# A two-layer decoder trunk with mixture of experts: the convolution's columns requested first, routing and gathering without the norm's scale and shift

## The chip, the cores and the metric

The kernel runs on one core of a Trainium2 chip. Its engines work side by side, each through its own instructions in order: TensorE (PE in the profile, its weight loads PEld), VectorE (DVE), ScalarE (ACT), GpSimd (POOL) and SyncE (SP), which here only issues transfers. ScalarE and GpSimd issue a few transfers too, in line with their other work. The metric is the device time of one execution in microseconds (us), as the median of several runs.

## What is computed

Two layers over 256 tokens of width 1024, all in float32. Layer 0 mixes tokens with a gated causal convolution of 31 taps, layer 1 with causal attention of 12 heads; in both, 4 more heads attend to 256 memory tokens. After each mixer stand an output projection, a residual with a norm, a mixture of 32 experts of which each token uses two, and a second residual with a norm.

```python
y = jnp.dot(jnp.concatenate([y_mix, y_mem], axis=-1), w_o[i])
x = layer_norm(DEEPNORM_ALPHA * x + y, ln1_g[i], ln1_b[i])
f = hierarchical_moe(x, w_rg[i], b_rg[i], w_re[i], b_re[i], w_gate[i], w_up[i], w_down[i])
x = layer_norm(DEEPNORM_ALPHA * x + f, ln2_g[i], ln2_b[i])
```

`layer_norm` is `(x - mean) * rsqrt(var + eps) * g + b`. The router takes the best of 4 groups and then the best two of its 8 experts; a token's output is the weighted sum of `silu(x @ w_gate) * (x @ w_up) @ w_down` over its two experts. Every expert has 6 MB of weights (three matrices of 2 MB), and all 32 are read in each layer: 403 of the 443 MB that the program reads.

## The kernel before

**Buffers and the order of loads.** Weights and large intermediate tiles share one pool, `big`, of 22 buffers of 128 x 2048 floats (1 MB each). `want` puts a load on a list, and `pump` hands the loads out in the order of that list, on SyncE's queue, as soon as the count of free buffers lets it; `act` takes a buffer for an intermediate tile and `free` gives it back; `done` gives back a weight tile. A buffer is given again as soon as it is free, in no fixed rotation. The list is: six tiles of convolution weights, the memory tokens, key and value weights, the four tiles of `w_o`, the gains and shifts of the first norm (`gb`, 1 MB: the 8 KB row repeated on 128 partitions), then the experts in the order of `_plan`, six tiles each (gate, up, down, two halves). Layer 1's list follows in the same manner. Eight semaphores are given in turn to all transfers that SyncE and ScalarE issue; a transfer that is given one in use waits at its issue until the earlier transfer on it has landed, and with it waits everything behind it on its engine.

**Static and dynamic experts.** Four experts (`s` in `_plan`) are fixed, so their 24 tiles can be loaded before the routing is known. The other 28 are taken in order of their token counts: their loads wait for the gate `("moe", l)`, opened when the router's result `eid` stands. `_plan` has twelve units, 0 to 11, each with one, two or four experts on 128 slots: two units with two static experts, then units of four, one, two, four, one, two, four, two, four and four experts.

**The start.** `raw` (the transposed x) comes in two halves. `parted` (L389) splits it into a rounded part, cast on ScalarE, and a remainder, subtracted on VectorE. `conv_layer` then takes its tile `cv_`, requests the per-channel columns (taps, bias, norm) into it on ScalarE's queue (L552), and begins to split the convolution's weights with `Feed` (L344 cast, L345 remainder) for the projection matmuls (L405). The gated product h goes to HBM and comes back in shifted copies `hs` (L597, L617, on GpSimd's queue); 28 of the 31 taps then run on TensorE (L626), three on VectorE (L607, L610). The token rows `xs` for the residual are loaded after the router's weights (L685, on SyncE) and multiplied into the accumulator by `residual` (L499 through L496).

**Norm and routing.** `moe` (L1043) takes the norm's statistics of token tile 0 (`norm_stats`), applies the norm with gains and shifts on VectorE (`norm_apply`, L519 and L520), then does the statistics of tile 1. `turn_tokens` transposes a tile for the router, `route` multiplies it by the router's weights (L1084) and adds a bias row (L1086), `choose` finds group and experts on VectorE (L1091 to L1106). Token tile 1 is already routed from rows without gains and shifts: its weights are `rwg`, the router's weights times the gains (GpSimd, L1049), and its bias row has the shifts' product added (L1135, L1144). GpSimd multiplies and adds gains and shifts to its two halves meanwhile (L1140, L1141). Then `Gather` multiplies the rows by one-hot matrices (L929) for the first unit; its result is copied from PSUM in two halves (L940). Later units do the same with `gather` (L950, copies at L952 through `evac`, which alternates ScalarE and VectorE).

**The experts.** For each expert, `gate` and `up` (L974), `turn` (L1004) and `down` (L1026); the next unit's gather stands between `up` and the previous expert's `down`. `scatter` adds a unit's result to the accumulator, and at the end of units 5, 6, 8 and 10 (`REST`) `residual` adds alpha times the normalised rows. After unit 11 comes the second norm.

## Time and profile before

| | |
|---|---|
| median of 3 runs | 1175.22 us (1174.49 to 1183.54) |
| the profiled execution | 1182.57 us, of it 1180.9 us span |
| mean granted TensorE clock | 0.947 |
| TensorE busy | 1028.2 us (87%), weight loads 722.3 us (61%) |
| VectorE, ScalarE, GpSimd busy | 366.4, 210.5, 60.6 us |
| moved by transfers | 447.16 MB, 379 GB/s over the span |

The span runs from the first to the last instruction. A row of a timeline gives start, duration, engine, line and operation with the tiles it writes and reads, merged where equal instructions follow each other; in brackets stands how long the engine was idle before it and what ended that. SPq and ACTq are transfer issues. A busy TensorE is not one at its peak, since matmuls are pipelined. PEclk is the share of the full clock that was granted: 1.00 is 2.4 GHz, 0.50 is 1.2 GHz.

### The profile page before, as it was taken

Reading aid. Unit: us, or ns where it says so; the run is one execution under the profiler, and the core shown is the slowest. Engines: PE = TensorE matmul, PEld = TensorE weight load, DVE = VectorE, ACT = ScalarE, POOL = GpSimd, SP = SyncE. Lnnn points to the kernel's source line nnn. Section 1 sums busy time; section 2 is a strip of 40 time slices with the busy share of each in tenths; the row PEclk is TensorE's granted clock in tenths of the full one; section 3 lists DMA queues with packets and bytes.
Section 4 is the critical chain, followed back from the end, with each engine's and each line's share of the span. In section 5 each row is a group of like instructions: output and inputs, shape, how many; then the busy total and the mean of one; then the engine's idle time right before and its main releaser. Section 6 shows DMA issues by size and latency. Waiting matters only on the chain. (4 is left out here: it accounts for less than half of the span.)

```text
span 1180.9 us, 26574 instructions
## 1 busy us (share of the span) xinstructions
PE 1028.2 (87%) x11292; PEld 722.3 (61%) x11292; DVE 366.4 (31%) x936; ACT 210.5 (18%) x456; POOL 60.6 (5%) x152
## 2 busy tenths in 40 slices
PE   1998999999889998866589998999997999996775
PEld 1986766665565575544469986666545656654542
DVE  3576832221121121111065765222211211221103
ACT  2314411111010010001044532011010111110000
POOL 1440200000000000000020002000000000000001
PEclk9999989999999999889899997999998999997777
DMA  9686969999999999999997386999999999999994
GB/s 381 235 282 265 347 251 419 424 424 426 425 424 425 427 424 425 426 426 425 425 427 271 108 293 252 384 425 424 426 427 422 425 427 425 424 426 425 426 425 177
DMA packets 63656, 447.16 MB, mean 379 GB/s; under 512 B 7656, under 2 KB 8040, under 8 KB 10280
## 3 DMA queue, kind: packets, MB, share of 16 engines
q1 hardware_dynamic: 61640, 439.73, 90.2%
q0 software_dynamic: 1600, 4.90, 1.5%
q8 instruction: 92, 1.51, 0.5%
q10 hardware_dynamic: 288, 0.73, 0.2%
q14 instruction: 36, 0.29, 0.1%
HBM read 442.87 MB, written 2.46 MB: 377 GB/s over the span
## 5 line engine op out<-in xcount | busy, mean ns | idle before, releaser
L974 PE MATMUL pb<-w,xg 128*32 128x128 f32 (+2 forms) x6528 | 400.1, 323 | 87.3 <-DMA w<-in_w_gate_dram 51.0
L974 PEld LDWEIGHTS pb<-w,xg 128*32 128x32 f32 (+2 forms) x6528 | 276.6, 123 | 208.9 <-issue 82.8
L1026 PE MATMUL pb<-w,hT 128*32 128x256 f32 (+1 forms) x1600 | 157.5, 432 | 7.8 <-DMA w<-in_w_down_dram 3.1
L1026 PEld LDWEIGHTS pb<-w,hT 128*32 128x32 f32 (+1 forms) x1600 | 74.5, 116 | 62.9 <-issue 36.5
L1031 ACT COPY o<-pb 32x256 f32<-32x256 f32 (+2 forms) x104 | 43.2, 416 | 367.1 <-DVE o L1031 232.5
L405 PE MATMUL pb<-xT,hl 128*128 128x256 f32 x672 | 86.0, 290 | 25.8 <-ACT hl L344 25.6
L1031 DVE COPY o<-pb 32x256 f32<-32x256 f32 (+2 forms) x104 | 49.8, 478 | 177.6 <-PE pb L1026 157.7
L998 DVE TENSOR_TENSOR h<-pb,h 128x128 f32<-128x128 f32 (+2 forms) x64 | 22.9, 358 | 253.8 <-PE pb L974 246.8
L405 PEld LDWEIGHTS pb<-xT,hl 128*128 128x128 f32 x672 | 84.0, 198 | 27.3 <-ACT hl L344 25.6
L496 PE MATMUL pa<-o,pt 128*128 128x512 f32 x192 | 92.7, 628 | 3.5 <-DVE o L1031 2.0
L950 PEld LDWEIGHTS pb<-oh,xn 128*128 128x128 f32 x704 | 80.6, 192 | 7.4 <-issue 7.4
L950 PE MATMUL pb<-oh,xn 128*128 128x128 f32 x704 | 84.0, 278 | 0.0
L345 DVE TENSOR_TENSOR hl<-w,hl 128x1024 fp32r<-128x1024 f32 x53 | 63.1, 1221 | 36.0 <-ACT hl L344 33.1
L496 PEld LDWEIGHTS pa<-o,pt 128*128 128x128 f32 x192 | 37.7, 207 | 44.5 <-issue 32.4
L344 ACT CAST hl<-w 128x1024 fp32r<-128x1024 f32 x54 | 54.7, 1053 | 33.3 <-DMA w<-in_memT_dram 19.3
L992 ACT ACTIVATE h<-pb 128x128 f32<-128x128 f32 (+2 forms) x64 | 21.2, 331 | 195.9 <-PE pb L974 195.0
L128 POOL TENSOR_SCALAR lmv<-lmv 128x1 f32<-128x1 f32 x8 | 1.7, 216 | 1027.7 <-DVE lmv L506 1026.0
L496 PE MATMUL pa<-hl,y 128*128 128x512 f32 x192 | 46.0, 395 | 0.0
L125 DVE COPY hT<-pb 128x128 f32<-128x128 f32 (+2 forms) x32 | 11.4, 358 | 105.1 <-PE pb L1004 81.2
L123 ACT COPY xg<-pb 128x512 f32<-128x512 f32 x22 | 12.9, 586 | 160.4 <-PE pb L950 160.4
L496 PEld LDWEIGHTS pa<-hl,y 128*128 128x128 f32 x192 | 35.5, 188 | 8.0 <-issue 0.5
L1238 DVE TENSOR_SCALAR ow<-iota,sm,sw 128x128 f32<-128x128 f32 x96 | 26.8, 343 | 19.2 <-PEq L1395 13.3
(229 smaller groups left out, 705.9 us busy)
## 6 DMA issues: line engine op xcount, KB each, us to landing
w<-in_w_gate_dram SPq DMA_DIRECT2D x128, 1024.0 KB, 19.5
w<-in_w_up_dram SPq DMA_DIRECT2D x128, 1024.0 KB, 19.5
w<-in_w_down_dram SPq DMA_DIRECT2D x128, 1024.0 KB, 19.5
w<-in_moba_w_in_dram SPq DMA_DIRECT2D x10, 1024.0 KB, 18.4
w<-in_w_o_dram SPq DMA_DIRECT2D x8, 1024.0 KB, 19.8
w<-in_conv_w_in_dram SPq DMA_DIRECT2D x7, 1024.0 KB, 15.4
w<-in_gains_dram SPq DMA_DIRECT2D x4, 1024.0 KB, 12.4
hs<-hd POOLq DMA_DIRECT2D x24, 142.0 KB, 3.2
```

The source lines that it names most:

```text
L123: nc.scalar.copy(o, i)
L344: nc.scalar.copy(hi, src)
L345: eng.tensor_sub(lo, src, hi.bitcast(F32))
L405: nc.tensor.matmul(o, lhsT=lhs(a, j), rhs=rhs(b, j), start=k == 0, stop=k == 3 * n - 1)
L496: nc.tensor.matmul(self.at[t][half], lhsT=lhsT, rhs=rhs, start=start, stop=stop)
L950: nc.tensor.matmul(p_[:, j - jj], lhsT=now(t, j), rhs=oh[t], start=t == 0, stop=t == NT - 1)
L974: nc.tensor.matmul(o_[b * n:(b + 1) * n, :], lhsT=self.xs[:, j, :], rhs=wj[:, pairs(b) if fw == P else slice(b * fw, (b + 1) * fw)], start ...
L992: nc.scalar.activation(self.h[:, :fw], g_, AF.Silu)
L998: nc.vector.tensor_mul(self.h[:, :fw], u_, self.h[:, :fw])
L1026: nc.tensor.matmul(ds[0][b * n:(b + 1) * n, :dw], lhsT=chunk(c), rhs=wd(c, b * dw, (b + 1) * dw), start=c == 0, stop=c == 3)
L1031: (nc.scalar.copy if 2 * b >= m else nc.vector.tensor_copy)(o[lo:lo + n, b * D // m:(b + 1) * D // m], ds[b] if nb == 1 else ds[0][b * n:( ...
L1238: nc.vector.tensor_scalar(o_[:, t], iota, sm[:, i:i + 1], sw[:, 4 + i:5 + i], op0=OP.is_equal, op1=OP.mult)
```

## The change

Five edits stand in it.

1. The tile `cv_` is taken, and the convolution's columns requested on ScalarE's queue, right after the two loads of `raw`.
2. The token rows `xs` are requested after the second `taps`, ahead of the last convolution block.
3. Both token tiles are normalised without gains and shifts (`plain`: half 0 on VectorE, half 1 on ScalarE). `rwg` is made in `router_load`; both tiles are routed with it and with the corrected bias row, whose product stands ahead of the first routing product. GpSimd's four operations on tile 1 are gone.
4. Gains and shifts are applied to the gathered, transposed copies, where they are one value per partition: `lift` reads PSUM in eight pieces of 128 x 128, four on ScalarE and four on VectorE, for each gather.
5. `gb` of the first norm is requested ahead of unit 7's experts. After unit 7 GpSimd makes `x1`, the rows with gains and shifts, in a buffer of its own (eight operations on 128 x 512), and `residual` reads it after units 8, 9, 9 and 10.

```diff
-REST = (5, 6, 8, 10)
+LIFT = 7
+REST = (8, 9, 9, 10)
...
     def want_moe(l):
-        for experts in plan:
+        for g, experts in enumerate(plan):
+            if g == LIFT:
+                want(("gb", l, 1), load_gb(2 * l))
...
+    cv_ = act("cv")
+    ncol = MC * (CW + 5), MC * 32
+    nc.scalar.dma_start(cv_[:, MC * S:MC * S + sum(ncol)], conv_cols)
     for b in range(3):
         for i in range(2):
             want(("cv", b, i), load(conv_w_in, 2 * b + i))
...
-    want(("gb", 0, 1), load_gb(0))
     want_moe(0)
...
-        rws.append((rw, rws_[:, 1], gbc))
+        rwg = rws_[:, 1]
+        nc.gpsimd.tensor_mul(rwg, rw, gbc[:, :J, None].to_broadcast([P, J, NL]))
+        rws.append((rw, rwg, gbc))
...
-        cv_ = act("cv")
...
-        nc.scalar.dma_start(cols, conv_cols)
...
         taps(1)
+        for t in range(NT):
+            for half in range(2):
+                nc.sync.dma_start(xn[t][half], xs[t, half])
         glu(2)
...
         router_load(0)
-        for t in range(NT):
-            for half in range(2):
-                nc.sync.dma_start(xn[t][half], xs[t, half])
         feed.ahead(2)
...
+    def lift(xg, p_, gbc, half):
...
+        for i in range(4):
+            j = 4 * half + i
+            g, b = gbc[:, j:j + 1], gbc[:, J + j:J + j + 1]
+            if half:
+                nc.vector.tensor_scalar(xg[:, j], p_[:, i], g, b, op0=OP.mult, op1=OP.add)
+            else:
+                nc.scalar.activation(xg[:, j], p_[:, i], AF.Identity, bias=b, scale=g)
...
-            evac(xg[:, jj:jj + 4], p_)
+            lift(xg, p_, gbc, jj // 4)
...
+        def plain(t):
...
+            nc.vector.tensor_scalar(xn[t][0], acc.at[t][0], mv[:, 0:1], mv[:, 2:3], op0=OP.subtract, op1=OP.mult)
+            nc.vector.scalar_tensor_tensor(mv[:, 3:4], mv[:, 0:1], -1.0, mv[:, 2:3], op0=OP.mult, op1=OP.mult)
+            nc.scalar.activation(xn[t][1], acc.at[t][1], AF.Identity, bias=mv[:, 3:4], scale=mv[:, 2:3])
...
-        gb = held(("gb", l, 1))
-        norm_apply(acc, 0, mv0, gb)
-        mv1 = norm_stats(acc, 1)
+        plain(0)
+        mv = norm_stats(acc, 1)
...
-        for half, eng in ((0, nc.gpsimd), (1, nc.gpsimd)):
-            o = xn[1][half]
-            g, b = gain(gb, half)
-            eng.tensor_mul(o, o, g)
-            eng.tensor_add(o, o, b)
-        done(("gb", l, 1))
...
+            if g == LIFT and end:
+                x1 = act("x1").rearrange("p (k d) -> p k d", k=4)
+                gb = held(("gb", l, 1))
+                for k in range(4):
+                    g_, b_ = gain(gb, k % 2)
+                    nc.gpsimd.tensor_mul(x1[:, k], xn[k // 2][k % 2], g_)
+                    nc.gpsimd.tensor_add(x1[:, k], x1[:, k], b_)
+                done(("gb", l, 1))
+            for k in range(4):
+                if g == REST[k] and end:
+                    residual(acc, k // 2, k % 2, x1[:, k])
```

ScalarE's first instructions before; `raw` is x, `hl` the split weights, and the brackets name the semaphores that a row waits for (DMAHW0 to DMAHW7 are the eight of the transfers):

```order
L394 ACT_TABLE_LOAD
L394 CAST xT<-raw 128x1024 [waits DMAHW0_49]
L552 DMA cv<-in_conv_cols_dram 128x408 [waits DMAHW0_49]
L344 CAST hl<-w 128x1024 [waits DMAHW2_49]
L344 CAST hl<-w 128x1024
L344 CAST hl<-w 128x1024 [waits DMAHW3_49]
```

and after, where the request waits for nothing and stands ahead of the casts:

```order
L254 DMA cv<-in_conv_cols_dram 128x408
L400 ACT_TABLE_LOAD
L400 CAST xT<-raw 128x1024 [waits DMAHW0_49]
L350 CAST hl<-w 128x1024 [waits DMAHW3_49]
L350 CAST hl<-w 128x1024
L350 CAST hl<-w 128x1024 [waits DMAHW4_49]
```

The request has moved from behind the wait for a transfer's semaphore to the head of the queue.

SyncE's queue from the four loads of `w_o` on, before; `xn` are the token rows, the rows of `gains` the 1 MB of the first norm:

```order
L183 DMA w<-in_w_o_dram 128x2048 x4
L189 DMA w<-in_gains_dram 128x2048
L213 DMA w<-in_w_gate_dram 128x2048 x2
L213 DMA w<-in_w_up_dram 128x2048 x2
L213 DMA w<-in_w_down_dram 128x2048 x2
L213 DMA w<-in_w_gate_dram 128x2048 x2
L327 DMA rbias<-in_b_rg_dram 1x4
L328 DMA rbias<-in_b_re_dram 1x32
L329 DMA rw<-in_w_r_dram 128x320
L331 DMA gbc<-in_gain_cols_dram 128x16
L685 DMA xn_72<-in_xs_dram 128x512
```

and after:

```order
L184 DMA w<-in_w_o_dram 128x2048 x4
L646 DMA xn_72<-in_xs_dram 128x512
L646 DMA xn_73<-in_xs_dram 128x512
L646 DMA xn_74<-in_xs_dram 128x512
L646 DMA xn_75<-in_xs_dram 128x512
L214 DMA w<-in_w_gate_dram 128x2048 x2
L214 DMA w<-in_w_up_dram 128x2048 x2
L214 DMA w<-in_w_down_dram 128x2048 x2
L214 DMA w<-in_w_gate_dram 128x2048 x2
L214 DMA w<-in_w_up_dram 128x2048
```

The token rows now stand right behind `w_o`, and the load of the gains has left this place.

VectorE from the statistics of token tile 0 (`lst`) to the first choice (`gm`, `gi`), before:

```order
L505 BN_STATS lst<-pa 128x6 x2
L506 BN_AGGR lmv<-lst 128x2
L519 SCALAR_TENSOR_TENSOR xn_72<-pa,lmv,w 128x512
L520 SCALAR_TENSOR_TENSOR xn_72<-xn_72,lmv,w 128x512
L519 SCALAR_TENSOR_TENSOR xn_73<-pa,lmv,w 128x512
L520 SCALAR_TENSOR_TENSOR xn_73<-xn_73,lmv,w 128x512
L505 BN_STATS lst<-pa 128x6 x2
L506 BN_AGGR lmv<-lst 128x2
L1128 SCALAR_TENSOR_TENSOR lmv<-lmv 128x1
L1130 TENSOR_SCALAR xn_74<-pa,lmv 128x512
L1077 COPY x1T<-pb 128x512
L1091 MAX gm<-lg 128x8
```

and after:

```order
L511 BN_STATS lst<-pa 128x6 x2
L512 BN_AGGR lmv<-lst 128x2
L1065 TENSOR_SCALAR xn_72<-pa,lmv 128x512
L1066 SCALAR_TENSOR_TENSOR lmv<-lmv 128x1
L511 BN_STATS lst<-pa 128x6 x2
L512 BN_AGGR lmv<-lst 128x2
L1065 TENSOR_SCALAR xn_74<-pa,lmv 128x512
L1066 SCALAR_TENSOR_TENSOR lmv<-lmv 128x1
L1151 TENSOR_TENSOR rows<-rbias,pb 1x40
L1096 COPY x1T<-pb 128x512
L1110 MAX gm<-lg 128x8
```

Four operations on tile 0 have become one with a small one behind it, and the bias row (`rows`) now stands ahead of the first choice.

## Rows read from the trace of the kernel before

**Rows 1.** The page, part 2: GB/s moved in 40 equal slices of the span.

```profile
GB/s 381 235 282 265 347 251 419 424 424 426 425 424 425 427 424 425 426 426 425 425 427 271 108 293 252 384 425 424 426 427 422 425 427 425 424 426 425 426 425 177
```

**Rows 2.** The chain that ended last: start us, us, what.

```profile
1143.53 19.41 DMA w<-in_w_down_dram
```

**Rows 3.** Timeline: start us, us, engine, line, what. The queue's release in layer 0.

```profile
160.00 3.02 SPq L213 DMA_DIRECT2D w<-in_w_down_dram  x2
```

**Rows 4.** Timeline of the start, with [idle before <-releaser].

```profile
9.40 0.33 SPq L183 DMA_DIRECT2D w<-in_conv_w_in_dram  x1
24.09 0.38 ACTq L552 DMA_DIRECT2D cv<-in_conv_cols_dram  x1
24.50 5.78 ACT L344 CAST hl<-w 128x1024 fp32r<-128x1024 f32 x6 [19.27 <-DMA w<-in_memT_dram]
25.60 31.77 PE L405 MATMUL pb<-xT,hl 128*128 128x256 f32 x240 [25.60 <-ACT hl L344]
```

**Rows 5.** Waits of the DMA queue's own engine, 0 to 30 us: us, times, longest.

```profile
SPq L183 <- DMA w<-in_conv_w_in_dram: 13.6, 6, 3.0
```

**Rows 6.** DMA issues: engine, count, KB each, median us to landing.

```profile
hs<-hd POOLq DMA_DIRECT2D x24, 142.0 KB, 3.2
cv<-in_conv_cols_dram ACTq DMA_DIRECT2D x1, 204.0 KB, 7.0
rw<-in_w_r_dram SPq DMA_DIRECT2D x2, 160.0 KB, 12.6
```

**Rows 7.** Timeline of the convolution: first shifted copies, first tap matmuls.

```profile
44.72 4.49 POOL L617 DMA_DIRECT2D hs<-hd  x8 [1.57 <-ACT hl L344]
57.30 3.01 PE L626 MATMUL pb<-hs,wdg 128*32 128x256 f32 x52
```

**Rows 8.** Timeline of layer 0's residual matmuls.

```profile
99.82 5.40 PE L496 MATMUL pa<-xn,alpha 128*128 128x512 f32 x8 [3.25 <-DMA xn<-in_xs_dram]
```

**Rows 9.** Timeline of layer 1's residual matmuls.

```profile
693.67 2.84 PE L496 MATMUL pa<-xn,alpha 128*128 128x512 f32 x6
```

**Rows 10.** Timeline of layer 0's routing, both token tiles.

```profile
142.91 0.74 PE L1135 MATMUL pb<-rw,gbc 128*1 128x40 f32 x16
144.16 1.10 DVE L1096 TENSOR_TENSOR pen<-iota,gi 128x4 f32<-128x4 f32 x1
145.19 1.26 POOL L1140 TENSOR_TENSOR xn<-xn,w 128x512 f32<-128x512 f32 x1
145.29 1.21 DVE L1098 SCALAR_TENSOR_TENSOR me<-pen,lg 128x32 f32<-128x32 f32 x1
147.06 0.81 DVE L1104 TENSOR_TENSOR m<-iota,ei 128x64 f32<-128x64 f32 x1
148.16 0.21 PE L1083 MATMUL pb<-msum,upper_b 128*128 128x32 bf16 x1 [3.06 <-DVE msum L1106]
149.76 3.78 PE L929 MATMUL pb<-oh,xn 128*128 128x128 f32 x16
150.57 0.16 DVE L1096 TENSOR_TENSOR pen<-iota,gi 128x4 f32<-128x4 f32 x1
150.77 0.19 DVE L1098 SCALAR_TENSOR_TENSOR me<-pen,lg 128x32 f32<-128x32 f32 x1
151.52 0.23 DVE L1104 TENSOR_TENSOR m<-iota,ei 128x64 f32<-128x64 f32 x1
```

**Rows 11.** The page, part 5: groups, busy us, mean ns of one.

```profile
L992 ACT ACTIVATE h<-pb 128x128 f32<-128x128 f32 (+2 forms) x64 | 21.2, 331 | 195.9 <-PE pb L974 195.0
L1238 DVE TENSOR_SCALAR ow<-iota,sm,sw 128x128 f32<-128x128 f32 x96 | 26.8, 343 | 19.2 <-PEq L1395 13.3
```

**Rows 12.** Waits of the DMA queue's own engine, 330 to 460 us.

```profile
SPq L213 <- PE pb L974: 1.2, 4, 0.4
```

**Rows 13.** Stretches: us, busy by engine, granted clock (PEclk), DMA share, GB/s.

```profile
150.00:152.00 2.00, 2.00 (x10) 2.00 (x11) 1.67 (x11) 0.45 (x3) 0.00 (x0) 0.50 0.93 348
714.00:716.00 2.00, 1.57 (x8) 1.53 (x8) 0.28 (x1) 0.94 (x3) 0.44 (x1) 0.62 1.02 430
```

More of the change, by code (lines that the diff above doesn't have):

```diff
@@ L496, in add, with residual @@
             nc.tensor.matmul(self.at[t][half], lhsT=lhsT, rhs=rhs, start=start, stop=stop)
-    def residual(acc, t, half):
-        acc.add(t, half, alpha, xn[t][half])
+    def residual(acc, t, half, x=None):
+        acc.add(t, half, alpha, xn[t][half] if x is None else x)
     def norm_stats(acc, t):
@@ L544, in conv_layer @@
         free()
-        cv_ = act("cv")
         cv = cv_[:, :MC * S].rearrange("p (c s) -> p c s", c=MC)
-        npc, nwr = MC * (CW + 5), MC * 32
-        cols = cv_[:, MC * S:MC * S + npc + nwr]
-        pct = cols[:, :npc].rearrange("p (c k) -> p c k", c=MC)
-        wrc = cols[:, npc:].rearrange("p (c b q) -> p c b q", c=MC, b=4)
+        cols = cv_[:, MC * S:MC * S + sum(ncol)]
+        pct = cols[:, :ncol[0]].rearrange("p (c k) -> p c k", c=MC)
+        wrc = cols[:, ncol[0]:].rearrange("p (c b q) -> p c b q", c=MC, b=4)
         id32 = cv_[:, 2048 - 32:]
-        nc.scalar.dma_start(cols, conv_cols)
         hd = dr.tile([MC, P * HW], F32, name="hd")
@@ L934, in tile, with get, gather @@
                 self.add(t, half)
-        def get(self, copy, xg=None):
-            if xg is None:
-                xg = xt([P, J, P], "xg")
+        def get(self, gbc):
+            xg = xt([P, J, P], "xg")
             for half in range(2):
-                copy(xg[:, 4 * half:4 * half + 4], self.ps[half].rearrange("p (j s) -> p j s", j=4))
+                lift(xg, self.ps[half].rearrange("p (j s) -> p j s", j=4), gbc, half)
             return xg
-    def gather(oh, xg=None):
+    def lift(xg, p_, gbc, half):
[6 more added lines that the diff above has]
+                nc.scalar.activation(xg[:, j], p_[:, i], AF.Identity, bias=b, scale=g)
+    def gather(oh, gbc, xg=None):
         if xg is None:
@@ L1084, in route @@
                 nc.tensor.matmul(p_[:, :NL], lhsT=x1T[t, j // 4][:, (j % 4) * P:(j % 4 + 1) * P],
-                                 rhs=(rwg if t else rw)[:, j, :], start=j == 0, stop=False)
+                                 rhs=rwg[:, j, :], start=j == 0, stop=False)
             nc.tensor.matmul(p_[:, :NL], lhsT=ident[0:1, 0:1].to_broadcast([1, P]),
-                             rhs=rows[0:1, :NL] if t else rbias, start=False, stop=True)
+                             rhs=rows[0:1, :NL], start=False, stop=True)
             nc.scalar.copy(lg[:, t], p_[:, :NL])
@@ L1126, in moe @@
         turn_tokens(0)
-        nc.vector.scalar_tensor_tensor(mv1[:, 3:4], mv1[:, 0:1], -1.0, mv1[:, 2:3], op0=OP.mult, op1=OP.mult)
-        nc.scalar.activation(xn[1][1], acc.at[1][1], AF.Identity, bias=mv1[:, 3:4], scale=mv1[:, 2:3])
-        nc.vector.tensor_scalar(xn[1][0], acc.at[1][0], mv1[:, 0:1], mv1[:, 2:3], op0=OP.subtract, op1=OP.mult)
-        route(0)
-        turn_tokens(1)
+        plain(1)
         p_ = pb()
@@ L1136, in moe @@
                              stop=j == J - 1)
-        for half, eng in ((0, nc.gpsimd), (1, nc.gpsimd)):
-            o = xn[1][half]
-            g, b = gain(gb, half)
-            eng.tensor_mul(o, o, g)
-            eng.tensor_add(o, o, b)
-        done(("gb", l, 1))
+        nc.vector.tensor_add(rows[0:1, :NL], rbias, p_[:1, :NL])
+        route(0)
+        turn_tokens(1)
         choose(0)
-        nc.vector.tensor_add(rows[0:1, :NL], rbias, p_[:1, :NL])
         route(1)
@@ L1201, in order @@
             nc.tensor.matmul(pid[:1, 32:33], lhsT=e32[:, 6:7], rhs=mhalf[:NE, 0:1], start=True, stop=True)
-        xgs[0] = xgs[0].get(nc.scalar.copy)
+        xgs[0] = xgs[0].get(gbc)
         def places():
@@ L1281, in one_more @@
                 sq = so[:, 4:8] if q else so[:, 0:4]
-                gather(one_hot(sq), xg=xo)
+                gather(one_hot(sq), gbc, xg=xo)
                 pt = spots_turned(spots(sq))
@@ L1379, in moe @@
             if nxt is not None:
-                xgs[g + 1] = gather(nxt)
+                xgs[g + 1] = gather(nxt, gbc)
             if i == len(flow) - 1:
@@ L1384, in moe @@
                 down(prev)
-            if g in REST and end:
-                t, half = divmod(REST.index(g), 2)
-                residual(acc, t, half)
+            if g == LIFT and end:
[9 more added lines that the diff above has]
+                    residual(acc, k // 2, k % 2, x1[:, k])
+                    if k == 3:
+                        free()
             prev = i
```

4 lines of the change are left out of this document (1 added, 3 removed).

## The prediction

> **What bounds the kernel now.** I read the transfer rate by slices first, then the chain that ended last, then the timelines of the places where the rate is low. The rate stands at 424 to 427 GB/s in most of the 40 slices; it is low in slices 2 to 6 (29 to 177 us: 235, 282, 265, 347, 251) and in slices 22 to 26 (620 to 767 us: 271, 108, 293, 252, 384) [rows 1]. Those are the two mixers with their routing, one for each layer. The chain ends in a run of weight loads; its last one takes 19.41 us [rows 2]. So the end is set by the bytes and by the time in which the transfer queue has nothing to do. That time ends, in each layer, when the first expert's first tile comes free: at 160.00 us the queue issues again, on a release by TensorE [rows 3]. Until then all 22 buffers are taken, before and after the change, by 22 weight tiles of the four static experts. From this follows the method: **a microsecond by which TensorE reaches the first expert earlier counts once, in either layer; a megabyte that moves from the idle time to behind it costs its transfer time.** 1024 KB at 425 GB/s is 2.47 us.
>
> **The start.** Before, ScalarE's queue holds: cast of x, request for the columns, casts of the first weights. The request goes out at 24.09 us, although ScalarE had nothing else to do for 19.27 us, and the first weight cast starts only at 24.50; TensorE's first matmul starts at 25.60, having waited 25.60 us for that cast [rows 4]. The request waits for a semaphore that the memory tokens' load (the eighth megabyte) used before it. The first weight tile itself had long landed: the load that reuses its semaphore is issued at 9.40 us [rows 4], and what that queue waited for in this stretch is the landing of convolution weights, six times, 13.6 us in all [rows 5]. After, the request is ScalarE's first instruction and waits for nothing; the next waits are those for x and for the first weight tile. The columns' 204 KB [rows 6] now stand ahead of that tile: 0.49 us at 425 GB/s. TensorE starts at 9.40 + 0.49 + (25.60 - 24.50) = 10.99 us, **14.6 us earlier**. It then has 31.77 us of matmuls without a stop [rows 4], five tiles that arrive at one per 2.47 us, so it is not starved.
>
> What is late next: the first shifted copies of h go through HBM, and their eight reads are issued in 4.49 us from 44.72 and land 3.2 us later [rows 6, 7], at 52.4; the taps start at 57.30 [rows 7], so there are 4.9 us to spare. Moved 14.6 us forward, they meet the initial loads, which fill the queue to about 40 us (some 16 MB) and, with the 1 MB of token rows that now follows them, to about 43. The columns' request met the full queue and took 7.0 us [rows 6]. If both the write and the reads took 3.8 us more, the taps would start 7.6 - 4.9 = 2.7 us late; if the reads overlap their own issue, not at all. I take 1.0 lost (0 to 2.7).
>
> **The token rows.** The four loads of xs move from behind the router's loads to right behind the output weights. Before, TensorE waits 3.25 us for them, and the eight residual matmuls then take 5.40 us [rows 8]; six of the same kind take 2.84 in layer 1 [rows 9], so eight would take 3.8. The wait alone is worth 3.25, wait and slow clock 4.85. I take 4.5, near the upper end, since both have the same cause; a little is kept back for VectorE's split of the next weights. On the queue they pass eight expert tiles and the four router loads; those come 1 MB later than they could, but they wait for buffers, not for the queue.
>
> **Routing.** In layer 0, VectorE's choice for token tile 0 runs beside GpSimd's four multiplies and adds of 1.26 us. L1096, L1098 and L1104 then take 1.10, 1.21 and 0.81 us, and 0.16, 0.19 and 0.23 for token tile 1, when GpSimd is idle; TensorE waits 3.06 us at the end of that choice [rows 10]. The change takes the four GpSimd operations away: 2.54 us off the path. Against it, the bias row (L1135, 0.74 us [rows 10]) now stands on TensorE ahead of the first routing product, of which about 0.5 is not hidden by the wait for the turned tokens. Net 2.0. The normalisation of tile 0 gets shorter too, but it ran beside the output projection of tile 1, so that is taken at zero (if it were not hidden, a gain of under 1). Layer 1 has the same pattern: **2.0 per layer**, 4.0 together.
>
> The router weights' product moves on GpSimd to right behind the router's loads. It waits for w_r, 12.6 us after its request [rows 6], and behind it stands the variance's power, needed some 19 us after that request: zero, with 3 us lost if the load took 6 us more.
>
> **The gather's copies.** Two copies of 128x512 become four ScalarE and four VectorE operations of 128x128. At 331 and 343 ns [rows 11] these are 1.3 and 1.4 us, the two engines side by side, where one half took about 0.6: at most 0.8 us later per gather. The first gather's ScalarE half lies under the second half's matmuls; in the other eleven a down projection stands between gather and next gate. Taken at zero; without cover it would be 12 x 0.8 = 10 us of TensorE per layer, which counts only where TensorE and not the queue is the limit.
>
> **Gains and x1.** The 1 MB of gains is no longer loaded in idle time (layer 0) or ahead of it (layer 1), but in the full stream ahead of unit 7: **+2.47 us per layer**, 4.9 together. It then holds a buffer until GpSimd has made x1, and x1 holds one up to unit 10. From 330 to 460 us the queue waited for TensorE 1.2 us in four waits [rows 12], so buffers are not short there: zero. GpSimd's eight operations (8 x 1.26 = 10 us) can make VectorE wait as above; the queue runs on meanwhile: zero. The four residuals only change units.
>
> **The sum.** -14.6 + 1.0 - 4.5 - 4.0 + 4.9 = **-17.2 us**. The profiled execution took 1182.6 us and would become 1165.4. It is 7.4 us above the median of the runs, 1175.2; from that median the forecast is **1158 us**.
>
> **Rivals.** (1) The clock. The granted clock is at its lower level, 0.50, after the 3.06 us wait, and each of the two first gathers of a layer takes 3.78 us for 16 matmuls [rows 10, 13]. If the shorter wait leaves the clock at 2.4 GHz, each gains 1.9: 3.8 per layer, 7.6 in all, 1150. Against it: layer 1's clock also falls (0.62 on the mean from 714 to 716) where TensorE shows busy 1.57 of 2 us with routing products and transposes alone [rows 13], and the change leaves all of these. The Trainium skill, "TensorE: Matmul & The Clock Gate", section "Part 1: The HAM clock gate", says that the throttled clock is the default and that activity of the array releases it; by it the removed idle time would keep the clock up and the time be 1150. The row from 714 us speaks against this, since the clock fell there without such a wait. (2) The early copies land late in all three convolution blocks: 3 x 2.7 = 8.1 instead of 1.0, 1165. (3) The start does not carry through, because something other than TensorE, a late slot or load, sets 160.00: 14.6 - 1.0 are lost, 1172. For it speaks only that the queue is full to 40 us. (4) Slower: one buffer less. If each of the 60 loads of units 8 to 10, in both layers, leaves the queue idle for 0.3 us, that is 36 us, 1194. It decides from 17.2 / 120 = 0.14 us per load on; the 1.2 us [rows 12] are far below that.
>
> **How the numbers follow.** Forecast 0.50, rival 1 0.22, rival 2 0.16, rival 3 0.07, rival 4 0.05. The range holds the forecast, both ends of its unknown terms, rivals 1 and 2 and most of the 7 us by which single executions differ: 1148 to 1170. About 1% (11.8 us, to 1163.5) is what a measurement of this kernel tells from no change. Faster by more: nearly all of the forecast (0.47), rival 1, half of rival 2: 0.77. Within 1%: the rest of these and rival 3: 0.18. Slower: 0.05.
>
> **What would show it.** TensorE's first matmul near 11 us, not 25.6; no wait for xs at the residuals; the three VectorE operations of the first choice near 0.2 us each; the queue's release by TensorE near 140 us instead of 160.0, and in layer 1 about 19.6 us earlier than before; one gains load in each expert stream. Wrong if the taps wait for shifted copies, if the rate falls below 420 GB/s between 200 and 600 us, or if the end moves less than the release in layer 1 less 2.5 us.

## The result, and the profile after

The changed kernel takes 1163.15 us (median of four runs, 1159.97 to 1164.06), the kernel before 1179.38 (four runs, 1174.49 to 1184.26). The ratio on record is 0.9844, 95% interval 0.9814 to 0.9874; the quotient of the two medians alone is 0.986. It is faster by 1.4 to 1.6%, more than the 1% that the prediction takes as told from no change. The forecast was 1158 us with a range of 1148 to 1170. The profiled execution after took 1159.97 us, its span is 1158.2 us against 1180.9, 22.7 us less.

The rate by slices, from part 2 of the page after:

```profile
GB/s 386 331 320 284 291 385 424 423 426 426 424 425 425 426 425 426 424 426 425 425 415 211 136 318 279 417 424 424 426 426 424 425 427 424 425 426 426 424 426 193
```

The low stretch of layer 0 is shorter and less deep than in [rows 1] (235 to 347 in five slices before; now 331, 320, 284, 291, 385), and the stream still stands at 423 to 427. Now the steps, in order of time; timelines read as in the rows of before. First the start, the first taps and the residuals:

```profile
0.85 0.40 ACTq L254 DMA_DIRECT2D cv<-in_conv_cols_dram  x1
10.20 23.98 PE L411 MATMUL pb<-xT,hl 128*128 128x256 f32 x180 [10.20 <-ACT hl L350]
44.85 4.92 PE L629 MATMUL pb<-hs,wdg 128*32 128x256 f32 x56 [3.47 <-DMA hs<-hd]
49.93 3.23 PE L629 MATMUL pb<-hs,wdg 128*32 128x256 f32 x56 [0.16 <-issue]
53.09 3.13 PE L411 MATMUL pb<-xT,hl 128*128 128x256 f32 x24
86.11 3.70 PE L502 MATMUL pa<-xn,alpha 128*128 128x512 f32 x8
```

TensorE starts at 10.20 us instead of 25.60 [rows 4]. But the taps now wait 3.47 us for the shifted copies and then run with the clock down (4.92 us for 56 matmuls, 3.23 for the next 56). The projection behind them starts at 53.09, in the kernel before at 63.48:

```profile
63.48 6.01 PE L405 MATMUL pb<-xT,hl 128*128 128x256 f32 x48
```

Of 15.4 us, 10.4 are left. The residuals no longer wait and end at 89.81 instead of 105.22 [rows 8]: 15.4 again.

Then the routing of layer 0 and the queue's release in both layers:

```profile
129.30 0.19 DVE L1117 SCALAR_TENSOR_TENSOR me<-pen,lg 128x32 f32<-128x32 f32 x1
130.06 0.22 DVE L1123 TENSOR_TENSOR m<-iota,ei 128x64 f32<-128x64 f32 x1
130.56 0.18 PE L1102 MATMUL pb<-msum,upper_b 128*128 128x32 bf16 x1 [0.86 <-DVE msum L1125]
131.71 3.39 PE L932 MATMUL pb<-oh,xn 128*128 128x128 f32 x16
135.72 2.05 PE L932 MATMUL pb<-oh,xn 128*128 128x128 f32 x16 [0.40 <-DVE oh L1131]
139.69 0.33 SPq L214 DMA_DIRECT2D w<-in_w_down_dram  x1
701.02 3.68 PE L932 MATMUL pb<-oh,xn 128*128 128x128 f32 x16
705.33 2.05 PE L932 MATMUL pb<-oh,xn 128*128 128x128 f32 x16 [0.40 <-DVE oh L1131]
709.30 3.02 SPq L214 DMA_DIRECT2D w<-in_w_down_dram  x2
```

Two of the three VectorE operations stand here with 0.19 and 0.22 us instead of 1.21 and 0.81, and TensorE's wait is 0.86 us instead of 3.06 [rows 10]. The release is at 139.69, 20.3 us earlier than 160.00 [rows 3]; in layer 1 it is at 709.30, 23.8 us earlier than 733.10. Last the gains' price: SyncE's first load for layer 1's attention and its last two expert loads, before (with layer 1's release between them) and then after.

```profile
573.12 0.34 SPq L183 DMA_DIRECT2D w<-in_moba_w_in_dram  x1
733.10 3.02 SPq L213 DMA_DIRECT2D w<-in_w_down_dram  x2
1141.11 2.75 SPq L213 DMA_DIRECT2D w<-in_w_down_dram  x2
```

```profile
555.21 0.34 SPq L184 DMA_DIRECT2D w<-in_moba_w_in_dram  x1
1119.40 2.79 SPq L214 DMA_DIRECT2D w<-in_w_down_dram  x2
```

From release to first attention load it was 413.1 us and is 415.5; from the second release to the last expert loads 408.0 and 410.1. Each layer's stream is 2.4 and 2.1 us longer.

### The profile page after: what moved, and what is told of

The parts are those of the page before. It is cut to its first block, busy times and chain, and to the rows that moved or that the text cites. A ratio compares the mean times of both kernels' runs of the same rounds, so it can differ in the third digit from the quotient of the medians.

```text
span 1158.2 us, 26720 instructions
## 1 busy us (share of the span) xinstructions
PE 1022.5 (88%) x11292; PEld 718.3 (62%) x11292; DVE 386.2 (33%) x1006; ACT 233.4 (20%) x528; POOL 71.1 (6%) x160
## 4 chain that ended last, share of the span: by engine, by line
DMA 51%; PE 20%; DVE 1%; issue 1%; ACT 1%; SPq 0%; DVEq 0%; ACTq 0%
DMA w<-in_w_up_dram 19%; DMA w<-in_w_down_dram 17%; DMA w<-in_w_gate_dram 15%; PE pb L987 5%; PE pb L411 5%; PE pa L502 3%; PE pb L1039 2%; PE pb L963 1%; PE pb L485 1%; PE pb L473 0%; PE pb L932 0%; PE pb L443 0%; PE pb L1017 0%; PE pb L388 0%; DVE xn L525 0%
## 5 line engine op out<-in xcount | busy, mean ns | idle before, releaser
L411 PE MATMUL pb<-xT,hl 128*128 128x256 f32 x672 | 85.4, 289 | 10.4 <-ACT hl L350 10.2
L502 PE MATMUL pa<-o,pt 128*128 128x512 f32 x192 | 88.3, 603 | 3.9 <-DVE o L1044 2.4
L351 DVE TENSOR_TENSOR hl<-w,hl 128x1024 fp32r<-128x1024 f32 x53 | 66.9, 1292 | 17.9 <-ACT hl L350 15.1
L954 ACT ACTIVATE xg<-pb,gbc 128x128 f32<-128x128 f32 x96 | 36.2, 457 | 151.9 <-PE pb L963 143.8
L952 DVE TENSOR_SCALAR xg<-pb,gbc 128x128 f32<-128x128 f32 x96 | 32.8, 405 | 72.5 <-PE pb L963 71.8
L126 DVE COPY hT<-pb 128x128 f32<-128x128 f32 (+2 forms) x32 | 11.4, 358 | 106.0 <-PE pb L1017 87.4
L1400 POOL TENSOR_TENSOR x<-xn,w 128x512 f32<-128x512 f32 x8 | 10.6, 1320 | 529.0 <-PE pb L1039 266.7
L1248 DVE TENSOR_SCALAR ow<-iota,sm,sw 128x128 f32<-128x128 f32 x96 | 35.0, 428 | 18.8 <-PEq L1415 12.9
```

Of the source, the lines that this page charges most:

```text
L351: eng.tensor_sub(lo, src, hi.bitcast(F32))
L411: nc.tensor.matmul(o, lhsT=lhs(a, j), rhs=rhs(b, j), start=k == 0, stop=k == 3 * n - 1)
L502: nc.tensor.matmul(self.at[t][half], lhsT=lhsT, rhs=rhs, start=start, stop=stop)
L952: nc.vector.tensor_scalar(xg[:, j], p_[:, i], g, b, op0=OP.mult, op1=OP.add)
L954: nc.scalar.activation(xg[:, j], p_[:, i], AF.Identity, bias=b, scale=g)
L1248: nc.vector.tensor_scalar(o_[:, t], iota, sm[:, i:i + 1], sw[:, 4 + i:5 + i], op0=OP.is_equal, op1=OP.mult)
```

## The experiments

"Release" is the start of the SyncE row that follows the long idle time at the routing, as above. The kernel before ran beside all of these, with medians of 1182.68 (20 runs), 1181.86 and 1182.48 us (9 runs each) on the three chips used. The ratios are those on record; a quotient of two medians differs from them by up to 0.002.

**Columns first, alone.** The kernel before with edit 1.

```diff
+    cv_ = act("cv")
+    ncol = MC * (CW + 5), MC * 32
+    nc.scalar.dma_start(cv_[:, MC * S:MC * S + sum(ncol)], conv_cols)
...
-        nc.scalar.dma_start(cols, conv_cols)
```

> The kernel before with only the request of the convolution's columns moved to the front. Theory: the start is worth 15.4 us at TensorE's first matmul (25.60 to about 10.2), but the first shifted copies meet the loads of w_o that still fill the queue, and the taps of the first block give back about 5.0 us of it; so the queue's release in layer 0 comes at 160.0 - 10.4 = 149.6 and the span is 10 us shorter than the 1180.9 of before. Rival A: the copies are late because of the token rows alone, which do not stand there in this kernel; then the release comes at 160.0 - 15.4 = 144.6. Rival B: something other than TensorE sets the release, and it stays above 155.

```profile
45.85 7.94 PE L627 MATMUL pb<-hs,wdg 128*32 128x256 f32 x112 [3.85 <-DMA hs<-hd]
91.23 5.40 PE L499 MATMUL pa<-xn,alpha 128*128 128x512 f32 x8 [4.41 <-DMA xn<-in_xs_dram]
151.41 0.33 SPq L213 DMA_DIRECT2D w<-in_w_down_dram  x1
```

1173.85 us, ratio 0.9934 (0.9912 to 0.9956); span 1170.5. The taps wait although no token rows stand in the queue, which rules out rival A. The release moved by 8.6 us, a little less than the 10.4 of the theory: 9.8 us are left at the projection behind the taps (53.72 against 63.48), and the token rows at their old place are now waited for 4.41 instead of 3.25 us.

**Routing, lift and gains alone.** The changed kernel with edits 1 and 2 undone; the loads of xs move back as in the next experiment's diff, and the columns so:

```diff
-    cv_ = act("cv")
...
-    nc.scalar.dma_start(cv_[:, MC * S:MC * S + sum(ncol)], conv_cols)
...
+        cv_ = act("cv")
...
+        nc.scalar.dma_start(cols, conv_cols)
```

> The kernel before with the routing, lift and gains edits, but with the columns' request and the token rows in their old places. Theory: the three VectorE operations of the first choice fall to about 0.2 us each, and the clock comes back earlier, so that layer 0's release comes 4.9 us earlier (155.1), layer 1's routing gives 6.0, and each layer pays 2.5 for its gains load: the release in layer 1 at 733.1 - 8.4 = 724.7 and the end 5.9 us earlier. Rival A: only the wait is saved, 2.0 per layer, and the other 3 to 4 us of the changed kernel's release came from the earlier start; then the releases stand at 158.0 and 733.1 - 1.5 = 731.6, and the end is 1 us later than before. Rival B: the gains load in the stream is hidden, and the end is 10.9 us earlier.

```profile
98.99 3.70 PE L500 MATMUL pa<-xn,alpha 128*128 128x512 f32 x8 [3.70 <-DMA xn<-in_xs_dram]
152.26 0.33 SPq L214 DMA_DIRECT2D w<-in_w_down_dram  x1
726.98 3.02 SPq L214 DMA_DIRECT2D w<-in_w_down_dram  x2
```

1180.76 us, ratio 0.9996 (0.9973 to 1.0019): no change that the times show, where the theory had 5.9 us. The profiled execution's span is 3.6 us shorter (1177.3). The release in layer 0 comes 7.7 us earlier, but 2.5 of that stand ahead of the routing: the residuals end at 102.69 instead of 105.22, mostly since their matmuls ran at the upper clock (3.70 instead of 5.40 us). From there to the release it is 49.6 us against 54.8 before: 5.2 gained. In layer 1 both gathers ran at the lower clock (3.78 us each). Its residuals start at 690.84, so from there to the release it is 36.1 us against 39.4 before [rows 9]: 3.3 gained, where the theory had 6.0. The share of the clock is thus not the same each time.

**Token rows back.** The changed kernel with edit 2 undone.

```diff
-        for t in range(NT):
-            for half in range(2):
-                nc.sync.dma_start(xn[t][half], xs[t, half])
         glu(2)
...
         router_load(0)
+        for t in range(NT):
+            for half in range(2):
+                nc.sync.dma_start(xn[t][half], xs[t, half])
```

> The changed kernel with the token rows requested behind the router's loads again. Theory: TensorE waits for them at the residuals again and loses 5.0 us there, while the wait of the taps for the first shifted copies (3.47 us in the changed kernel) stays, since the loads of w_o cause it: release in layer 0 at 139.7 + 5.0 = 144.7, and the time 5 us above the changed kernel's. Rival A: the token rows cause the wait of the taps; it goes, 5.0 us come back there, and the release stays near 139.7. Rival B: with the earlier start the rows have time to land anyway; no wait at the residuals, release 139.7 with the taps' wait unchanged.

```profile
45.45 7.94 PE L629 MATMUL pb<-hs,wdg 128*32 128x256 f32 x112 [3.71 <-DMA hs<-hd]
91.82 6.74 PE L502 MATMUL pa<-xn,alpha 128*128 128x512 f32 x8 [5.41 <-DMA xn<-in_xs_dram]
151.06 0.33 SPq L214 DMA_DIRECT2D w<-in_w_down_dram  x1
```

1169.61 us, ratio 0.9904 (0.987 to 0.9939). The taps' wait stays, as the theory says. The residuals end at 98.56 instead of 89.81: the edit is worth 8.7 us here, not the 5.0 of the theory, since with the earlier start the wait is 5.41 us and the matmuls run at the lower clock. The release is 11.4 us later; the rest lies between residuals and release, most of it in the two gathers (3.78 us each, at the lower clock, against 3.39 and 2.05).

**First block's copies ahead.** The changed kernel with the first eight reads on SyncE, and w_o with all behind it after them.

```diff
-        want(("wo", 0, b), load(w_o, b))
+        want(("wo", 0, b), load(w_o, b), "hs0")
...
+            if b == 0:
+                opened("hs0")
...
-                    nc.gpsimd.dma_start(hs[c]...
+                    (nc.gpsimd if n else nc.sync).dma_start(hs[c]...
```

> The changed kernel with the eight reads of the first shifted copies issued by SyncE instead of GpSimd, and the four loads of w_o (and all behind them) requested after these reads. Theory: the reads meet a nearly empty queue (11 MB are requested ahead of them, landed by about 28 us), land by about 33, and the taps of the first block do not wait: the next projection starts near 48.1 instead of 53.09, and the release in layer 0 comes 5.0 us earlier, at 134.7; the time falls 5 us below the changed kernel's. Rival A: w_o, the token rows or the second block's copies come late in turn, and the release stays within 1 us of 139.7. Rival B: the taps do not wait but the clock is at its lower level there anyway, so that only 3.5 us come: 136.2.

```profile
41.51 6.25 PE L631 MATMUL pb<-hs,wdg 128*32 128x256 f32 x112
76.01 4.92 PE L631 MATMUL pb<-hs,wdg 128*32 128x256 f32 x56 [2.61 <-DMA hs<-hd]
140.52 0.33 SPq L214 DMA_DIRECT2D w<-in_w_down_dram  x1
```

1163.05 us, ratio 0.9841 (0.9811 to 0.9871): nothing gained. The outcome is that of rival A, through copies that it does not name. The first taps do not wait and start at 41.51, but the third block's reads now meet the experts' loads: 2.61 and 0.50 us of waiting and 4.92 instead of 3.23 us of matmuls. 3.3 us gained at the first taps, 5.4 at the projection behind them (47.69), are 0.5 at the residuals (85.65 against 86.11), and the second gather ran at the lower clock (3.78 us).

**All copies ahead.** The same with all three blocks' reads on SyncE, and the static experts' loads opened behind the third block's.

```diff
+            if b != 1:
+                opened(f"hs{b}")
...
-                             None if kind == "s" else ("moe", l))
+                             ((None, "hs2")[l == 0] if kind == "s" else ("moe", l)))
```

> The changed kernel with the reads of all three blocks' shifted copies on SyncE's queue: w_o behind the first block's, the experts' loads behind the third block's. Theory: no taps wait for copies (the first block's reads pass 11 MB, the others 5 MB that land before them), the 4.5 us that the third block lost with only the first copies ahead do not come, the residuals of layer 0 start 5.0 us earlier than in the changed kernel (86.11 to 81.1), and the release follows to 134.7 where the gathers' clock is as in the changed kernel, 136.5 where it is low: time 4 to 5 us below the changed kernel's. Rival: the experts' loads, now requested about 12 us later, are late themselves: the first expert waits for its weights or the router's weights come after TensorE needs them, and the release stays near 139.7 or comes later.

```profile
41.01 6.25 PE L631 MATMUL pb<-hs,wdg 128*32 128x256 f32 x112
80.55 3.70 PE L502 MATMUL pa<-xn,alpha 128*128 128x512 f32 x8
134.72 0.33 SPq L214 DMA_DIRECT2D w<-in_w_down_dram  x1
```

1157.49 us, ratio 0.9801 (0.9773 to 0.9829), 4.9 us below the changed kernel on the same chip (next run). No taps wait, and the release comes at 134.72 where the theory had 134.7. The residuals start 5.6 us earlier; 0.5 of it goes again in a wait for VectorE right behind them. So the 5.0 us lost at the start were lost to loads that nothing needed yet. The queue of the reads and the order of the loads were changed together, so what either is worth alone is not shown.

**The changed kernel again.**

> The changed kernel once more, unedited, for a second profiled execution. Theory: the copies' wait, the token rows and the waits of VectorE are the same to 0.3 us, but where TensorE's clock falls is not: of the two first gathers of each layer any takes between 2.05 and 3.8 us, the way they differ between the kernels run so far (3.39 and 2.05 in the changed kernel, 3.18 and 3.78, 3.78 and 3.78, 3.21 and 2.15 in kernels with the same routing), and so the releases of the two layers lie up to 2.5 us behind the first profile's (139.7 and 709.3). Rival: the clock follows the instructions alone; both releases come back within 0.5 us.

```profile
44.95 3.23 PE L629 MATMUL pb<-hs,wdg 128*32 128x256 f32 x56 [3.36 <-DMA hs<-hd]
49.69 3.23 PE L629 MATMUL pb<-hs,wdg 128*32 128x256 f32 x56 [1.50 <-DMA hs<-hd]
```

1162.42 us, ratio 0.9857 (0.9827 to 0.9886). The releases are at 139.18 and 709.66, both within about 0.5 us of the first profile: the rival's number, in this kernel. The clock did not fall at the taps this time, and the second read was waited for instead (1.50 us); the loss is nearly the same, so it is the transfers', not the clock's. The gathers took 3.34, 2.05, 3.57 and 2.05 us.

**A filler in the wait.** The changed kernel with two unused matmuls ahead of L1102.

```diff
                 if t and j == J - 2:
+                    fill = pb()
+                    for _ in range(2):
+                        nc.tensor.matmul(fill, lhsT=ident, rhs=xn[0][0], start=True, stop=True)
```

> The changed kernel with two matmuls of 128x128 by 128x512 without use on TensorE, in the 0.86 us in which it waits for the first choice (0.46 us each by the residuals' row). Theory of the first rival of the prediction: the wait is what lowers the clock; without it the first gather takes 2.05 us instead of 3.39 and 3.68, and the releases come about 1.4 us earlier in each layer. Rival, by the row of before in which the clock fell without a wait: the small routing products before the wait lower it, the gathers keep 3.2 to 3.8 us and the releases stay or come up to 0.3 us later.

```profile
129.48 1.96 PE L1104 MATMUL pb<-xn,ident 128*128 128x512 f32 x4
132.20 2.05 PE L932 MATMUL pb<-oh,xn 128*128 128x128 f32 x16
135.26 2.05 PE L932 MATMUL pb<-oh,xn 128*128 128x128 f32 x16 [0.44 <-DVE oh L1134]
```

The same stretch by windows (us, busy by engine, granted clock, DMA share, GB/s), changed kernel and then with filler:

```profile
132.00:134.00 2.00, 2.00 (x10) 2.00 (x10) 1.72 (x12) 0.40 (x3) 0.00 (x0) 0.50 1.00 414
```

```profile
132.00:134.00 2.00, 2.00 (x18) 1.95 (x19) 1.30 (x11) 0.58 (x3) 0.00 (x0) 1.00 0.87 369
```

1160.64 us, ratio 0.9828 (0.9797 to 0.9859). The clock stays at 1.00 and all four gathers take 2.05 us. The rival is out: the small products, which are all still there, do not lower the clock by themselves. The filler both takes the idle time away and puts dense matmuls in its place; which of the two keeps the clock up is not shown. The expectation had the filler's size wrong: a row of x4 is two such matmuls, each 0.98 us and not 0.46. So it overran the 0.86 us wait, the next product started 0.7 us later (131.28 against 130.56), and the releases (139.23 and 708.54) gained only 0.5 and 0.8 us against the first profile of the changed kernel, none and 1.1 us against the second.

**GpSimd's work back.** The changed kernel with four multiplications beside the first choice.

```diff
         turn_tokens(1)
+        scr = ot([P, 512], "scr")
+        nc.gpsimd.tensor_mul(scr, xn[1][0], x1T[1, 0])
+        for _ in range(3):
+            nc.gpsimd.tensor_mul(scr, xn[1][0], xn[1][1])
         choose(0)
```

> The changed kernel with four GpSimd multiplications of 128x512 beside the first choice, into a tile that nothing reads: the cover that the change took away, and nothing else of it. Theory: VectorE's three operations take 0.8 to 1.2 us again, the choice is about 2.5 us longer, and the release comes 2.5 us later in each layer (142.2 and about 714) if the second gather keeps 2.05 us, about 4.2 us later (143.9) if the longer wait also moves the fall of the clock onto both gathers (3.78 each), as in the kernel before. Rival: the three operations stay at 0.2 us, so that it was not GpSimd's work beside them that made them long, and the releases stay within 0.5 us.

```profile
130.13 0.19 DVE L1117 SCALAR_TENSOR_TENSOR me<-pen,lg 128x32 f32<-128x32 f32 x1
130.16 4.00 POOL L1157 TENSOR_TENSOR scr<-xn,xn 128x512 f32<-128x512 f32 x3
130.89 0.64 DVE L1123 TENSOR_TENSOR m<-iota,ei 128x64 f32<-128x64 f32 x1
132.89 0.19 PE L1102 MATMUL pb<-msum,upper_b 128*128 128x32 bf16 x1 [2.57 <-DVE msum L1125]
```

1169.08 us, ratio 0.9899 (0.9867 to 0.993). The wait of TensorE is 2.57 us. From the residuals' end to the release it is 52.4 us in layer 0 (release at 142.86) against 49.9 in the changed kernel, 2.5 more with the second gather at 2.05; in layer 1, from the start of its residuals, 37.6 against 33.4, 4.2 more with both gathers at 3.78. Both numbers are the theory's two cases. Which VectorE operations are stretched depends on what GpSimd runs at that moment: L1117, which started between two of its operations, kept 0.19 us. Of the three that the expectation names the others took 0.37 and 0.64 us; most of the longer wait is the sum behind them (L1125), 1.27 us instead of 0.19.

**Plain copies of the gathered rows.**

```diff
...
-            if half:
-                nc.vector.tensor_scalar(xg[:, j], p_[:, i], g, b, op0=OP.mult, op1=OP.add)
-            else:
-                nc.scalar.activation(xg[:, j], p_[:, i], AF.Identity, bias=b, scale=g)
+        (nc.vector.tensor_copy if half else nc.scalar.copy)(xg[:, 4 * half:4 * half + 4], p_)
```

> The changed kernel with the gathered rows copied as they are, one operation of 128x512 for each half instead of four of 128x128; the norm's scale and shift are left out of the experts' input. Theory: the eight smaller operations cost nothing, since they lie under matmuls; both releases come within 0.5 us of the changed kernel's and the time is the same within 1 us. Rival: they are on TensorE's path, at 0.8 us per gather; then the release comes 0.8 us earlier, and the 22 later gathers of both layers together give up to 17 us where TensorE limits.

1164.70 us, ratio 0.9846 (0.9814 to 0.9877): the lift costs nothing that the time shows. In layer 1 it is 33.3 us from residuals to release against 33.4. In layer 0 the release came 2.95 us later, at 142.64, which is not the copies' doing: both gathers ran at the lower clock there (3.78 us each).

**Four megabytes more.** The changed kernel with four more loads of gains per layer ahead of unit 7.

> The changed kernel with four more loads of 1 MB per layer, of the gains again, ahead of unit 7's experts; nothing reads them and their buffers come back where the first one's does. Theory: a load in the full stream costs its transfer time, 2.47 us, so 9.9 us per layer: the first load of layer 1's attention weights moves from 555.2 to 565.1, the release in layer 1 from 709.3 to 719.2, and the span from 1158.2 to 1178. Rival A: loads there are hidden behind TensorE, and the span stays within 2 us. Rival B: the five buffers held until GpSimd is done leave the queue without a free one, and a megabyte costs clearly more, over 14 us per layer.

```profile
565.15 0.34 SPq L184 DMA_DIRECT2D w<-in_moba_w_in_dram  x1
1142.03 2.76 SPq L214 DMA_DIRECT2D w<-in_w_down_dram  x2
```

One execution, span 1180.5 us, 22.3 more for 8 MB. From the releases (140.33 and 720.93) on, the streams are 424.8 and 421.1 us long against 415.5 and 410.1: 2.3 and 2.8 us per megabyte. Theory, and neither rival; the rest of the 22.3 lies outside the streams (0.6 at the first release, 1.7 in layer 1's attention).

**The kernel before again.**

> The kernel before once more, unedited, for a second profiled execution; its own times lie between 1174.5 and 1185.8 us. Theory: the starts and routings are the same to 1 us (releases near 160.0 and 733.1), as all four first gathers run at the clock's lower level and the waits for the token rows and VectorE are fixed; what differs between executions is where the clock falls in the experts' stretches and how long the stream from the release to its last load takes (413 and 411 us in the first profile). Rival: the wait for the token rows or the routing differs by several us between executions, and the profiled one, 7 us above the median, was one with the longer waits.

```profile
100.66 5.83 PE L496 MATMUL pa<-xn,alpha 128*128 128x512 f32 x8 [4.96 <-DMA xn<-in_xs_dram]
```

1183.83 us (one execution), span 1182.2. The wait for the token rows was 4.96 us instead of 3.25, and the release came 1.4 us later, at 161.37; all four first gathers took 3.75 to 3.78 us. So neither answer is quite right: one wait does vary by 1.7 us, but no execution of 1174 to 1178 us was profiled. What sets these apart stays open.

**The best of both.** All copies ahead, and one filler instead of two.

> The kernel with all three blocks' shifted copies on SyncE's queue, and one matmul of 128x128 by 128x512 without use (about 0.98 us, half of the 1.96 us that two took) on TensorE while it waits for the first choice. Theory: one fills the 0.86 us wait and adds 0.1 us to it, and the clock stays at its upper level as it did with two, so that the first gathers take 2.05 us instead of 3.44 and 3.63: release in layer 0 at 133.4 instead of 134.72, in layer 1 about 2.8 us earlier than 705.4, and the time 2 to 3 us below the 1157.5 us of the kernel without the filler. Rival: with one the clock falls all the same, as the small products are still there; the gathers keep 3.4 to 3.7 us and the time stays.

```profile
125.01 1.10 PE L1104 MATMUL pb<-xn,ident 128*128 128x512 f32 x2
126.97 2.05 PE L934 MATMUL pb<-oh,xn 128*128 128x128 f32 x16
134.00 0.33 SPq L214 DMA_DIRECT2D w<-in_w_down_dram  x1
703.99 0.33 SPq L214 DMA_DIRECT2D w<-in_w_down_dram  x1
```

1154.60 us, ratio 0.9756 (0.9735 to 0.9777): faster than the kernel before and the changed one, and 2.9 us below the kernel without filler, which ran on another chip (their ratios' intervals overlap from 0.9773 to 0.9777). One filler is enough to keep the clock up in both layers. The releases gained 0.7 and 1.4 us, half of what was expected.

## Why the prediction was right, and where its terms were not

The mechanism held: the residuals' 15.4 us reached the release in full, with the routing's gain on top, and the end moved with the release in layer 1, less one gains load. Of the prediction's three signs of being wrong one came: the taps wait for shifted copies. The rate stays at 424 GB/s or more in stretches of 20 us from 200 to 600 us, and the end moved 22.7 us, the release in layer 1 less 2.5 us 21.3. The sum against the two profiled executions:

| term | predicted | measured |
|---|---|---|
| start | -14.6 | -15.4 |
| first copies late | +1.0 | +5.0 |
| token rows | -4.5 | -5.0 |
| routing, layer 0 | -2.0 | -4.9 |
| gains load, layer 0 | +2.47 | +2.4 |
| routing, layer 1 | -2.0 | -5.9 |
| gains load, layer 1 | +2.47 | +2.1 |
| end, from the last expert loads on | 0 | -1.0 |
| sum | -17.2 | -22.7 |

That the release in layer 0 came at 139.69, where the terms give 139.9, is partly luck: the copies cost 4.0 us more than predicted, while the routing gave 2.9 us more, and start and token rows 1.3 together. The column is one pair of executions. By the medians of the runs, the columns alone give 8.8 us (1182.68 to 1173.85), the edits of routing, lift and gains on top of them 4.2 (1169.61), and the token rows about 6 more (19.4 in all when the changed kernel ran again). Without the earlier start the routing edits gave 1.9 us, which is within the noise.

**Start.** The columns' 204 KB did not delay the first weights: the load that reuses their semaphore is issued at 9.10 us (9.40 before), so the 0.49 us in the sum did not come.

**First copies: the term was mis-sized.** The prediction had write and reads take up to 3.8 us more each, overlap some of it, and took 1.0 of a bound of 2.7. The write took that, but the reads much more. Transfers issued from 24 to 40 us after, and from 40 to 55 us before (count, KB each, median us to landing):

```profile
hs<-hd POOLq DMA_DIRECT2D x8, 142.0 KB, 11.4
hd<-h POOLq DMA_DIRECT2D x2, 144.0 KB, 6.0
```

```profile
hs<-hd POOLq DMA_DIRECT2D x8, 142.0 KB, 3.0
hd<-h POOLq DMA_DIRECT2D x4, 144.0 KB, 2.1
```

Eight reads that land in 3.0 us on an idle queue took 11.4 behind w_o and the token rows (11.2 behind w_o in the kernel with the columns alone): 3.9 and 8.4 us more against the 4.9 us of slack, part of it under the reads' own issue. The bound came from the columns' 7.0 us [rows 6], one transfer of 204 KB, and was no bound for eight small reads. Only the first block paid (rival 2 had all three), until the third block's turn came in the kernel with the first copies ahead.

**Token rows.** 5.0 us in the sequence of the table. The split is not additive: with the earlier start the old place would have cost 8.7 us (the run with the token rows back), so start and copies alone bring 8.6 (the kernel with the columns alone) to 10.4 at the release, and moving the token rows the rest.

**Routing: mis-sized by the clock.** In layer 0 VectorE's first choice, from its first MAX8 to the sum, went from 4.41 to 1.87 us: 2.54, the prediction's number. The bias row cost 0.35 (0.5 predicted). That is a net of 2.2 against 2.0. The other 2.7 came from TensorE running faster: the second gather at 2.05 instead of 3.75, and steps of about 0.5 each in the products ahead of the first gather and in the first gather itself. Rival 1 asked for the clock to stay up through both gathers. It fell all the same, but came back before the second one:

| kernels | gathers at the routing, us |
|---|---|
| routing of before (before, again, columns alone) | 12 of 12 at 3.75 to 3.78 |
| changed routing, no filler (changed kernel twice, all copies ahead, four more, routing alone, token rows back, first copies ahead, plain copies) | first gathers 3.18 to 3.78; second 2.05 to 2.15 in 11 of 16, 3.78 or 3.79 in 5 |
| changed routing with GpSimd's work back | first gathers 3.78; second 2.05 and 3.78 |
| with filler (two kernels) | 8 of 8 at 2.05 |

So without filler and without GpSimd's work the routing is worth 2.1 to 3.6 us per layer where the second gather runs at the lower clock and 4.3 to 6.2 where the clock has come back for it. The prediction set against rival 1 the row from 714 us [rows 13], where it says that the clock fell without such a wait. That reading was wrong. TensorE had idled 0.57 us right ahead of its work there:

```profile
714.43 1.90 PE L1075 MATMUL pb<-ident,xn 128*128 128x128 f32 x8 [0.57 <-DVE xn L1130]
```

The granted clock is 1.00 in the microsecond before 714, 0.74 in the one from 714 and 0.50 in the one from 715. So the row speaks against rival 1 for another reason than the one given: a wait far shorter than the 3.06 us was followed by the fall too, and the change left 0.86 us. The filler shows that with these 0.86 us filled the clock stays up, with the same small products before it. The Trainium skill's page "TensorE: Matmul & The Clock Gate", section "Part 1: The HAM clock gate", says that activity releases the throttle; the filler's rows agree.

**Lift, gains, buffers.** The lift at zero is confirmed (1164.70 against 1162.42 and 1163.15 us). The gains' 2.47 us per megabyte measured 2.1 to 2.8. (In the stretch of [rows 12] the queue's waits for TensorE are 1.8 us in six, with those on L950 and L1026.) Rival 4's shortage of buffers would have shown as a longer stream; the streams grew by 2.4 and 2.1 us, one gains load each.

**Rival 3** fell with the release: 15.4 us at the residuals are in the 20.3 at the release in full.

**The number.** 1158 was the median of three runs less 17.2 us. The sum was short by 5.5 us against the profiled pair. The three runs of before (1175.22) were low as well: later medians were 1181.9 to 1182.7. From these, 17.2 us give about 1165, and 1162 to 1163 was measured. The two errors partly cancelled: that 1158 came as close as it did is in part luck.

## What to carry to other kernels

When a start is moved forward, price each small transfer that used to find an idle queue by the loads that it will now meet, and count eight small ones as eight, not by one larger one. Loads without a reader for a long time belong behind such transfers, in all places at once: held back for one only, they collide with the next. Before a short dense stretch on TensorE, look for the idle time ahead of it; here one unused matmul of 1 us in a wait of 0.9 us was worth 1.4 and 1.6 us at the gather behind it, and 0.7 and 1.4 us at the release.

## What the runs showed of the hardware that was not expected

- The clock after a short wait: with TensorE idle for 0.86 us behind small products the granted clock fell to 0.50 and the gather took 3.2 to 3.8 us; with that wait filled it stayed at 1.00 and the gather took 2.05. A wait of 0.69 us behind 48 matmuls of the projection (it ends at 77.66 us in the changed kernel) left it at 1.00. Kernels with the same routing instructions differed in when it came back (11 of 16 second gathers).
- GpSimd beside VectorE: VectorE's operations on two SBUF tiles took 0.37 to 1.27 us when a GpSimd multiplication ran beside them, and 0.16 to 0.29 otherwise; one that started just before such a multiplication kept 0.19, and MAX8 beside the same multiplications kept 0.16 to 0.20. The Trainium skill's "GPSIMD Engine Reference", section "8. Key points", names contention with VectorE instructions of two SBUF inputs; the rows agree.
- Reads of 142 KB on GpSimd's queue took 3.0 us alone, 11.4 us with w_o and the token rows (5 MB) requested ahead of them on SyncE's queue, and 11.2 us with w_o alone.
